# Two heads split at once, and doubled or laid over by transfers inside SBUF: the keys and queries of a two-layer decoder kernel

## The chip, the cores and the metric

The kernel runs on one core of one Trainium2 chip. The metric is the device time of one execution in microseconds, smaller is better; three executions are compared by their median. The chip is trn2 throughout. The engines are TensorE (PE in the rows; PEld is its weight load), VectorE (DVE), ScalarE (ACT), GpSimd (POOL) and SyncE (SP, which here issues the transfers).

## What is computed

Two layers of a hybrid decoder on one sequence of 512 tokens, 1024 wide, in fp32. Each layer projects the normalized input to three groups of heads of 64: 4 heads of forgetting attention, 8 query heads of native sparse attention (NSA, on 2 key groups, with compressed, selected and window branches) and 4 heads of dilated attention. Cut to what matters here:

```python
proj = h @ w_in
(fq, fk, fv, ff, nq, kc, vc, ks, vs, kw, vw, ng, dq, dk, dv) = jnp.split(proj, splits, axis=-1)
o_fox = fox_attention(heads(fq, 4), heads(fk, 4), heads(fv, 4), log_f)
o_nsa = nsa_attention(rope(nq, 8), rope(kc, 2), ..., rope(ks, 2), ..., rope(kw, 2), ...)
o_dil = dilated_attention(rope(dq, 4), rope(dk, 4), heads(dv, 4))
x = x + rms_norm(concat(o_fox, o_nsa, o_dil) @ w_out, attn_post_norm)
x = x + rms_norm(conv_ffn(rms_norm(x, ffn_pre_norm), ...), ffn_post_norm)
```

Scores are `q . k * 64**-0.5`, then masks, softmax and values.

## The kernel before

Tokens lie in four blocks of 128 (`NST`). Every factor of a matmul that must be exact is split into a high and a low part, each in the reduced fp32 form that TensorE takes at its full rate: `hi` is a rounding copy on ScalarE, `lo = x - hi` is a subtraction on VectorE (for some weights on GpSimd). A projection is hi·hi + hi·lo + lo·hi, in blocks of 12 matmuls (`s_mms`, through `mm` at line 115). Weights of a layer come in by loads of 512 KB that SyncE issues (`load`, line 134) into a pool of three raw tiles.

A score needs the product of a query head (64 channels) with a key head. The 128 rows of the array hold the query twice over, its high part in partitions 0 to 63 and its low part in 64 to 127; a key head is therefore needed **doubled**, the same 64 channels in both halves, and in two planes, high and low. A score is then two matmuls (`st_scores`): query tile by high plane, query tile by low plane.

How the tiles come about: a projection leaves tokens on partitions. `staged` (lines 718 to 743) copies each token block to a row buffer with the rotary turn (`rope`, lines 465 to 477); for keys it writes every head twice, side by side. `turn` (735 to 738) transposes 128 columns of the four token blocks into one PSUM tile, four transposes of 128x128 (tag `pt`, two buffers). For queries such a block holds two heads, for keys one head doubled. `keep` then calls `q_evac` (485 to 492: for each of the two heads one ScalarE copy of 64x512 with the scale into the upper half of the tile and one VectorE subtraction into the lower half) or `k_evac` (494 to 498: one ScalarE copy and one VectorE subtraction of 128x512 for the one doubled head). The forgetting heads' keys `fk` (525 to 543) are made in the same way, through `t_block` (479 to 483), and their queries `fq` straight from a projection that leaves channels on partitions, with `q_evac`.

Row buffers (`rt`) come from one pool of ten, which the attention rows of the units below use too.

The order around the change: the scores are cut into units (lines 1074 to 1079) of one head, branch and query block: units 0 to 15 forgetting, 16 to 79 NSA (head 0 branch `ks` is 16 to 19, head 0 branch `kw` 20 to 23), 80 to 95 dilated. The slot loop (1240 to 1251) runs one unit per slot through nine stages, each with its lag (`LAGS`), and between them takes `step`s of the projections still open, at the rate of a fixed table (`RATE`), on which pieces such as `evac`, `turn` and `keep` hang with delays (`EV`). `operands` (1081), called first in `st_scores`, takes steps until the query and key tiles of its unit are there (`until`, 1074). TensorE's order is this order of the program.

Of the kernel before, what the change touches and what calls it, by code (L numbers as in the profile page):

```python
# [10 lines left out]
F32R = mybir.dt.float32r  # L11
# [63 lines left out]
def tile_hybrid_block(  # L75
# [26 lines left out]
    def bt(shape, dt=F32, name="b"):  # L102
        return big.tile(shape, dt, tag="b", name=nm(name))
# [344 lines left out]
    for l in range(DEPTH):  # L448
# [43 lines left out]
            return q  # L492

        def k_evac(p):
            k = bt([128, 2, 512], F32R, "k")
            nc.scalar.activation(k[:, 0, :], p, AF.Copy)
            nc.vector.tensor_sub(k[:, 1, :], p, f(k[:, 0, :]))
            return k

        def new_v(nh=2):  # L500
            return bt([128, 8 // nh, nh, 2, 64], F32R, "v")
# [23 lines left out]
        for s in range(NST):  # L525
            if s % 2 == 0:
                for c in range(2):
                    for u in range(s, s + 2):
                        s_mms(sl256(pk_, u), u, range(4 * c, 4 * c + 4), wk[c], c == 0 and u % 2 == 0,
                              c == 1 and u % 2 == 1)  # L530
            p = ps("s")[:, 0:284]
            for c, (k0, k1) in enumerate(((0, 3), (3, 6), (6, 8))):
                s_mms(p, s, range(k0, k1), wv[c], c == 0, c == 2)
            if s == 1:
                turn_pair(1, 0, l, HT2)
            v_evac(fv[s // 2], s % 2, p[:, 0:256])
            nc.vector.tensor_add(zz[:, s, :], p[:, 256:284], bias)
            d = rt((128, 4, 2, 64))
            nc.scalar.activation(d, bc(hd(sl256(pk_, s)), 2, 2), AF.Copy)
            tl.append(d.rearrange("p h u d -> p (h u d)"))  # L540
        tmode.__exit__(None, None, None)
        store["fv"] = fv
        store["fk"] = [k_evac(t_block(tl, 128 * j)) for j in range(4)]
        cpar = small.tile([128, 2, 88], F32, tag="cpar", bufs=1, name=nm("cpar"))
        crow = rt((88, 2, 128))
        for j in range(3):
# [171 lines left out]
        def staged(key, turned, dup, nh, v=None, plain=0):  # L718

            tl = []  # L720

            def evac(s, p):
                w = nh * 64 * (2 if dup else 1)
                d = rt((128, w + plain))
                rope(d[:, 0:w].rearrange("p (h u d) -> p h u d", h=nh, d=64), hd(p[:, 0:64 * nh]), s, nh)
                if plain:
                    nc.scalar.activation(d[:, w:w + plain], p[:, 64 * nh:64 * nh + plain], AF.Copy)
                if v is not None:
                    if s == 0:
                        store[v] = new_v()  # L730
                    v_evac(store[v], s, p[:, 64 * nh:64 * nh + 128])
                tl.append(d)

            def turn(j):
                p = ps(TT)
                for s in range(NST):
                    nc.tensor.transpose(p[:, 128 * s:128 * s + 128], tl[s][:, 128 * j:128 * j + 128], ident)  # L737
                pieces.later(EV[3], keep, p)

            def keep(p):  # L740
                store.setdefault(key, []).append((k_evac if dup else q_evac)(p))

            return evac, [(turn, j) for j in range(nh * (2 if dup else 1) // 2)]

        def dv_evac(s, p):
            if s == 0:
# [353 lines left out]

        state, whole = {"o": None, "p": None}, []

        def st_scores(u):
            t = u["t"]
            n = u["n"] = 128 * (t + 1)
# [131 lines left out]
        with tc.manual_schedule(engines={mybir.EngineType.PE}):  # L1237
            for i in range(FIRST):
                step()
            for i in range(len(units) + LO):  # L1240
                slot[0] = i
                U = lambda lag: units[i - lag] if 0 <= i - lag < len(units) else None
                for lag, fn in stages:
                    if U(lag) is not None:
                        fn(U(lag))
# [177 lines left out]
```

## Time and profile before

| what | us |
|---|---|
| median of 3 runs (1368.1 to 1369.65) | 1369.39 |
| the profiled execution's own time | 1369.85 |
| its span | 1367.9 |
| mean granted TensorE clock | 0.998 of full |

The profile is of one execution. Its time stands 1.95 us above its span and 0.46 us above the median. The span has per layer one stage of projections and attention (about 40 to 310 us in layer 0, 710 to 985 us in layer 1) and one of output projection and feed-forward. The page gives engine totals, the chain that ended last and the costliest groups; the timelines, the waits and the transfers tell where in the program something happens.

### The profile page before, as it was taken

What the parts mean: (1) busy time and instruction counts of PE and PEld (TensorE: products, weight loads), DVE (VectorE), ACT (ScalarE), POOL (GpSimd) and SP (SyncE); (2) the same over time, 40 slices, a digit from 0 to 9 for tenths busy, and PEclk for the clock granted to TensorE, in tenths of its full rate; (3) what the DMA queues carried; (4) which work ended last, traced back from release to release, by engine and by line L of the source; (5) the groups of instructions that cost most, each with busy time, mean ns of one, the idle gap of its engine ahead of it and who ended that gap; (6) DMA issues with size and microseconds to landing.
All of it is one profiled execution on the core that took longest, in us unless ns stands there. A gap on an engine that the chain in (4) does not pass through costs nothing.

```text
span 1367.9 us, 21028 instructions
## 1 busy us (share of the span) xinstructions
PE 1338.0 (98%) x7855; PEld 1177.9 (86%) x7855; DVE 850.4 (62%) x1893; ACT 728.2 (53%) x1506; POOL 287.0 (21%) x343
## 2 busy tenths in 40 slices
PE   9999999999999999999999999999999999999997
PEld 8899998978888888888898999999798888888886
DVE  7677787677755555433464887777876555554334
ACT  6567767777533333333465677667774333333232
POOL 2364753341000000000004647634210000000000
PEclk9999999999999999999999999999999999999999
DMA  6323311131333333333333242111323333332231
GB/s 181 94 63 115 104 35 48 58 128 33 107 93 103 97 92 96 104 93 123 111 96 93 63 139 63 47 41 58 120 62 98 103 92 93 104 97 92 94 122 62
DMA packets 145517, 123.74 MB, mean 90 GB/s; under 512 B 8264, under 2 KB 135688, under 8 KB 145416
## 3 DMA queue, kind: packets, MB, share of 16 engines
q1 hardware_dynamic: 145416, 122.40, 29.5%
q8 instruction: 62, 1.02, 0.3%
q14 instruction: 39, 0.32, 0.1%
HBM read 118.19 MB, written 4.19 MB: 89 GB/s over the span
## 4 chain that ended last, share of the span: by engine, by line
PE 85%; DVE 7%; ACT 4%; POOL 2%; issue 2%; DMA 0%; SPq 0%; ACTq 0%; POOLq 0%; DVEq 0%
PE acc L115 39%; PE s L115 19%; PE pt L115 13%; PE o L115 10%; PE pt L1156 3%; POOL wt L795 1%; PE pt L737 1%; DVE hl L271 1%; DVE pl L1172 1%; DVE r L1126 1%; ACT r L1131 1%; DVE x L913 0%; ACT hh L270 0%; ACT h L310 0%; ACT ph L1167 0%
## 5 line engine op out<-in xcount | busy, mean ns | idle before, releaser
L154 DVE TENSOR_TENSOR wl_up<-raw_up,wh_up 128x1024 fp32r<-128x1024 f32 x78 | 95.6, 1225 | 170.8 <-ACT wh_up L146 170.8
L146 ACT ACTIVATE wh_up<-raw_up 128x1024 fp32r<-128x1024 f32 (+1 forms) x90 | 89.6, 1001 | 160.4 <-PE acc L115 68.1
L154 DVE TENSOR_TENSOR wl_wd<-raw_wd,wh_wd 128x1024 fp32r<-128x1024 f32 x42 | 51.5, 1225 | 133.7 <-ACT wh_wd L146 133.7
L146 ACT ACTIVATE wh_wd<-raw_wd 128x1024 fp32r<-128x1024 f32 x42 | 44.5, 1060 | 144.8 <-PE pt L115 135.5
L1143 POOL TENSOR_SCALAR r<-r,sm,gates 128x128 f32<-128x128 f32 (+3 forms) x128 | 86.4, 683 | 126.1 <-DVE sm L1139 82.3
L1131 ACT ACTIVATE r<-r,sm 128x128 f32<-128x128 f32 x192 | 106.7, 557 | 9.3 <-DVE sm L1126 8.4
L115 PE MATMUL acc<-hh,wl_up 128*128 128x512 f32 (+1 forms) x272 | 102.4, 376 | 0.0
L115 PE MATMUL acc<-hl,wh_up 128*128 128x512 f32 (+1 forms) x272 | 102.4, 376 | 0.0
L115 PE MATMUL acc<-hh,wh_up 128*128 128x512 f32 (+1 forms) x272 | 102.4, 376 | 0.0
L150 POOL TENSOR_TENSOR wl_kc<-raw_kc,wh_kc 128x512 fp32r<-128x512 f32 x8 | 11.8, 1490 | 417.6 <-ACT wh_kc L146 416.8
L115 PE MATMUL s<-k,q 128*128 128x512 f32 (+3 forms) x384 | 96.2, 337 | 0.6 <-DVE sm L1126 0.6
L1172 DVE TENSOR_TENSOR pl<-pt,ph 128x384 fp32r<-128x384 f32 x144 | 85.6, 596 | 17.3 <-ACT ph L1167 15.9
L1167 ACT ACTIVATE ph<-pt 128x384 fp32r<-128x384 f32 x144 | 75.4, 523 | 29.1 <-PE pt L1156 27.9
L1126 DVE CUSTOM_DVE_ANT_0 r<-s,cmask 128x128 f32<-128x128 f32 (+3 forms) x160 | 76.0, 482 | 20.6 <-PE s L115 16.2
L1156 PE MATMUL pt<-ident,r 128*128 128x128 f32 x480 | 77.5, 276 | 7.0 <-DVE pl L1172 5.5
L115 PE MATMUL acc<-wh_wd,gh 128*128 128x512 f32 x252 | 83.7, 389 | 0.0
L115 PE MATMUL s<-hh,wh_up 128*128 128x512 f32 (+1 forms) x224 | 80.4, 359 | 0.0
L115 PE MATMUL s<-hl,wh_up 128*128 128x512 f32 (+1 forms) x224 | 80.4, 359 | 0.0
L115 PE MATMUL s<-hh,wl_up 128*128 128x512 f32 (+1 forms) x224 | 80.4, 359 | 0.0
L1347 ACT ACTIVATE r<-r 128x512 f32<-128x512 f32 x44 | 27.8, 632 | 85.7 <-DVE r L1328 85.5
L1156 PEld LDWEIGHTS pt<-ident,r 128*128 128x128 f32 x480 | 55.4, 141 | 15.9 <-POOL r L1143 6.8
L115 PE MATMUL acc<-wh_wo,mix 128*128 128x256 f32 (+1 forms) x296 | 67.6, 305 | 0.0
(439 smaller groups left out, 4121.2 us busy)
## 6 DMA issues: line engine op xcount, KB each, us to landing
raw_up<-in_w_up_dram SPq DMA_DIRECT2D x88, 512.0 KB, 3.8
raw_wd<-in_w_down_dram SPq DMA_DIRECT2D x44, 512.0 KB, 3.4
raw_wo<-in_w_out_dram SPq DMA_DIRECT2D x16, 512.0 KB, 3.5
x<-in_x_dram SPq DMA_DIRECT2D x8, 512.0 KB, 5.9
raw_nq<-in_w_in_dram SPq DMA_DIRECT2D x8, 512.0 KB, 3.7
raw_w<-in_cmp_w_k_dram SPq DMA_DIRECT2D x8, 512.0 KB, 4.0
raw_w<-in_cmp_w_v_dram SPq DMA_DIRECT2D x8, 512.0 KB, 4.2
raw_fk<-in_w_in_dram SPq DMA_DIRECT2D x4, 512.0 KB, 5.9
```

What stands on the lines that cost most here:

```text
L115: nc.tensor.matmul(o, lhsT=lhsT, rhs=rhs, start=start, stop=stop, skip_group_check=True)
L146: nc.scalar.activation(hi[:, ks], raw[:, ks], AF.Copy)
L154: nc.vector.tensor_sub(lo[:, ks], raw[:, ks], f(hi)[:, ks])
L271: nc.vector.scalar_tensor_tensor(lo, src, gain[:, k:k + 1], f(hi), op0=ALU.mult, op1=ALU.subtract)
L737: nc.tensor.transpose(p[:, 128 * s:128 * s + 128], tl[s][:, 128 * j:128 * j + 128], ident)
L1126: nc.vector.tensor_tensor_reduce(row[:, 0:n], u["S"][:, 0:n], u["mask"][:, 512 - n:512], op0=ALU.add, op1=ALU.min, scale=1.0, scalar=3.0e3 ...
L1131: nc.scalar.activation(row[:, 0:n], row[:, 0:n], AF.Exp, scale=-1.0, bias=sm_[0], accum_out=sm_[1])
L1143: nc.gpsimd.tensor_scalar(row[:, 0:n], row[:, 0:n], z["sm"][2], g_, op0=ALU.mult, op1=ALU.mult)
L1156: nc.tensor.transpose(p[:, 128 * c:128 * c + 128], blocks[z], ident)
L1167: nc.scalar.activation(hi, src, AF.Copy)
L1172: nc.vector.tensor_sub(*u["lo"])
L1347: nc.scalar.activation(cd[0], cd[0], AF.Silu)
```

## The change

Keys are no longer written twice side by side: the row buffers of `fk` and of `staged` hold each head once, a turned block holds two key heads, and half as many key blocks are turned. `k_evac` makes two key tiles from one block: one ScalarE copy and one VectorE subtraction of 128x512 into the second tile, then three transfers of 64x1024 (256 KB each) on SyncE's queue: the first head from the upper half of the second tile to both halves of the first, and then the second head from its lower half to its upper half. `q_move` replaces `q_evac` for the NSA and dilated queries: one ScalarE copy and one VectorE subtraction of 128x512 into two row buffers, then four transfers of 64x512 (128 KB each) that lay high and low parts of the two heads over each other in the query tile; `fq` keeps `q_evac`. `ask` takes the steps for the operands of a unit with the first query block one slot earlier, for NSA and dilated units.

```diff
--- before.py
+++ after.py
@@ -492,10 +492,26 @@
             return q
 
         def k_evac(p):
-            k = bt([128, 2, 512], F32R, "k")
-            nc.scalar.activation(k[:, 0, :], p, AF.Copy)
-            nc.vector.tensor_sub(k[:, 1, :], p, f(k[:, 0, :]))
+
+            k = [bt([128, 2, 512], F32R, "k") for _ in range(2)]
+            own, other = slice(64, 128), slice(0, 64)
+            nc.scalar.activation(k[1][:, 0, :], p, AF.Copy)
+            nc.vector.tensor_sub(k[1][:, 1, :], p, f(k[1][:, 0, :]))
+            for h in (other, own):
+                nc.sync.dma_start(f(k[0])[h], f(k[1])[other])
+            nc.sync.dma_start(f(k[1])[other], f(k[1])[own])
             return k
+
+        def q_move(p):
+
+            hi, lo = rt(dt=F32R), rt(dt=F32R)
+            nc.scalar.activation(hi, p, AF.Copy, scale=-0.125)
+            nc.vector.scalar_tensor_tensor(lo, p, -0.125, f(hi), op0=ALU.mult, op1=ALU.subtract)
+            q = bt([128, 2, 512], F32R, "q")
+            for j in range(2):
+                for i, part in enumerate((hi, lo)):
+                    nc.sync.dma_start(f(q)[64 * i:64 * i + 64, j, :], f(part)[64 * j:64 * j + 64, :])
+            return [q]
 
         def new_v(nh=2):
             return bt([128, 8 // nh, nh, 2, 64], F32R, "v")
@@ -535,12 +551,12 @@
                 turn_pair(1, 0, l, HT2)
             v_evac(fv[s // 2], s % 2, p[:, 0:256])
             nc.vector.tensor_add(zz[:, s, :], p[:, 256:284], bias)
-            d = rt((128, 4, 2, 64))
-            nc.scalar.activation(d, bc(hd(sl256(pk_, s)), 2, 2), AF.Copy)
-            tl.append(d.rearrange("p h u d -> p (h u d)"))
+            d = rt((128, 256))
+            nc.scalar.activation(d, sl256(pk_, s), AF.Copy)
+            tl.append(d)
         tmode.__exit__(None, None, None)
         store["fv"] = fv
-        store["fk"] = [k_evac(t_block(tl, 128 * j)) for j in range(4)]
+        store["fk"] = [k for j in range(2) for k in k_evac(t_block(tl, 128 * j))]
         cpar = small.tile([128, 2, 88], F32, tag="cpar", bufs=1, name=nm("cpar"))
         crow = rt((88, 2, 128))
         for j in range(3):
@@ -720,7 +736,7 @@
             tl = []
 
             def evac(s, p):
-                w = nh * 64 * (2 if dup else 1)
+                w = nh * 64
                 d = rt((128, w + plain))
                 rope(d[:, 0:w].rearrange("p (h u d) -> p h u d", h=nh, d=64), hd(p[:, 0:64 * nh]), s, nh)
                 if plain:
@@ -738,9 +754,9 @@
                 pieces.later(EV[3], keep, p)
 
             def keep(p):
-                store.setdefault(key, []).append((k_evac if dup else q_evac)(p))
-
-            return evac, [(turn, j) for j in range(nh * (2 if dup else 1) // 2)]
+                store.setdefault(key, []).extend((k_evac if dup else q_move)(p))
+
+            return evac, [(turn, j) for j in range(nh // 2)]
 
         def dv_evac(s, p):
             if s == 0:
@@ -1100,6 +1116,11 @@
 
         state, whole = {"o": None, "p": None}, []
 
+        def ask(u):
+            if u["t"] == 0 and u["grp"] != "f":
+                operands(u)
+
+
         def st_scores(u):
             t = u["t"]
             n = u["n"] = 128 * (t + 1)
@@ -1240,6 +1261,8 @@
             for i in range(len(units) + LO):
                 slot[0] = i
                 U = lambda lag: units[i - lag] if 0 <= i - lag < len(units) else None
+                if i + 1 < len(units):
+                    ask(units[i + 1])
                 for lag, fn in stages:
                     if U(lag) is not None:
                         fn(U(lag))
```

How the change moves instructions, at three places of layer 0. The first is TensorE around the first score of unit 16 (`s<-k,q` with the query tile of the first two NSA heads; `kw` is the projection of the window keys, L737 in the program before and L753 in the changed one are the transposes of `turn`). Before:

```order
L115 MATMUL acc_1525<-wh_kw_229_1365,hl_94 128x256
L737 MATMUL pt_1598<-ident,r_1417 128x128
L737 MATMUL pt_1598<-ident,r_1449 128x128
L737 MATMUL pt_1598<-ident,r_1498 128x128
L737 MATMUL pt_1598<-ident,r_1546 128x128
L115 MATMUL s_1608<-k_1341,q_1603 128x128 x2
L115 MATMUL acc_1525<-wh_kw_229_1365,hh_89 128x256
L115 MATMUL acc_1525<-wl_kw_230_1366,hh_89 128x256
```

And now:

```order
L115 MATMUL acc_1494<-wh_kw_227_1356,hl_94 128x256
L753 MATMUL pt_1567<-ident,r_1405 128x128
L753 MATMUL pt_1567<-ident,r_1437 128x128
L753 MATMUL pt_1567<-ident,r_1486 128x128
L753 MATMUL pt_1567<-ident,r_1515 128x128
L115 MATMUL s_1581<-k_590,q_720 128x512 x2
L115 MATMUL s_1581<-cst,esel 128x512
L1177 MATMUL pt_1595<-ident,r_1382 128x128 x4
L115 MATMUL s_1600<-k_1328,q_1576 128x128 x2
L115 MATMUL acc_1494<-wh_kw_227_1356,hh_89 128x256
```

The second turn of the NSA queries now comes ahead of the scores of unit 15 (three matmuls into `s_1581`) and of the transposes of four rows (L1177), and unit 16's score, which read its query straight behind the turn, now comes behind these. Between the first turn and the second stand 12 matmuls of `kw` in both.

The second place is SyncE's queue in the same part of the program, with the loads of weights (`raw_w` of the compression, `raw_nq` of the second half of the NSA queries). Before:

```order
L134 DMA raw_w_0_2_286_1650<-in_cmp_w_k_dram 128x4x256
L134 DMA raw_w_0_3_298_1694<-in_cmp_w_k_dram 128x4x256
L134 DMA raw_nq_0_309_1753<-in_w_in_dram 128x4x256
L134 DMA raw_w_1_0_316_1809<-in_cmp_w_v_dram 128x4x256
L134 DMA raw_w_1_1_324_1838<-in_cmp_w_v_dram 128x4x256
L134 DMA raw_nq_1_329_1876<-in_w_in_dram 128x4x256
L134 DMA raw_w_1_2_357_2000<-in_cmp_w_v_dram 128x4x256
L134 DMA raw_w_1_3_364_2028<-in_cmp_w_v_dram 128x4x256
```

And now:

```order
L134 DMA raw_w_0_3_299_1690<-in_cmp_w_k_dram 128x4x256
L513 DMA q_1576<-r_1572 64x512
L513 DMA q_1576<-r_1573 64x512
L513 DMA q_1576<-r_1572 64x512
L513 DMA q_1576<-r_1573 64x512
L513 DMA q_1628<-r_1624 64x512
L513 DMA q_1628<-r_1625 64x512
L513 DMA q_1628<-r_1624 64x512
L513 DMA q_1628<-r_1625 64x512
L134 DMA raw_nq_0_305_1731<-in_w_in_dram 128x4x256
L134 DMA raw_w_1_0_312_1787<-in_cmp_w_v_dram 128x4x256
L134 DMA raw_w_1_1_320_1816<-in_cmp_w_v_dram 128x4x256
```

The transfers of keys (L501, L502) and queries (L513) stand between the loads: the load of `raw_nq` now comes behind eight of them, which wait for ScalarE's and VectorE's halves of two query pairs.

The third place is TensorE around unit 20, the first with window keys (`w_1_0` is a weight of the compression, `nq` the second half of the NSA query projection). Before:

```order
L115 MATMUL acc_1875<-wl_w_1_0_326_1841,wth_1383 128x256
L737 MATMUL pt_1892<-ident,r_1744 128x128
L737 MATMUL pt_1892<-ident,r_1769 128x128
L737 MATMUL pt_1892<-ident,r_1801 128x128
L737 MATMUL pt_1892<-ident,r_1825 128x128
L115 MATMUL s_1900<-k_1897,q_1603 128x128 x2
L115 MATMUL s_1900<-k_1897,q_1603 128x256 x2
L1156 MATMUL pt_1921<-ident,r_1639 128x128
L1156 MATMUL pt_1921<-ident,r_1672 128x128 x2
```

And now (L1177 is the transposes of the rows; between the two pieces stand eleven more matmuls of `nq`):

```order
L115 MATMUL acc_1853<-wl_w_1_0_322_1819,wth_1374 128x256
L115 MATMUL acc_1853<-wh_w_1_0_321_1818,wth_1374 128x256
L115 MATMUL acc_1853<-wl_w_1_0_322_1819,wth_1374 128x256
L115 MATMUL s_1877<-k_1328,q_1576 128x512 x2
L1177 MATMUL pt_1890<-ident,r_1604 128x128 x4
L115 MATMUL acc_1815<-wh_nq_0_313_1789,hh_89 128x256
L115 MATMUL acc_1815<-wl_nq_0_314_1790,hh_89 128x256
L115 MATMUL acc_1815<-wh_nq_0_313_1789,hl_93 128x256
...
L115 MATMUL acc_1815<-wl_nq_0_314_1790,hh_90 128x256
L115 MATMUL acc_1815<-wh_nq_0_313_1789,hl_94 128x256
L115 MATMUL s_1907<-k_1870,q_1576 128x128 x2
```

The first score of unit 20 stood right behind the second turn of the window keys. There is one turn now, further ahead, and between it and that score stand the matmuls with `w_1_0`, the scores of unit 19, four transposes and twelve matmuls of `nq`.

## Rows read from the trace of the kernel before

**Rows 1.** The page, part 1: busy time, its share of the span and the number of instructions of each engine.

```profile
PE 1338.0 (98%) x7855; PEld 1177.9 (86%) x7855; DVE 850.4 (62%) x1893; ACT 728.2 (53%) x1506; POOL 287.0 (21%) x343
```

**Rows 2.** The page, part 4: the chain of work that ended last, shares of the span by engine.

```profile
PE 85%; DVE 7%; ACT 4%; POOL 2%; issue 2%; DMA 0%; SPq 0%; ACTq 0%; POOLq 0%; DVEq 0%
```

**Rows 3.** The waits of TensorE over the whole span: who waited, for whom, microseconds in total, how many times, the longest.

```profile
PE pt L1156 <- DVE pl L1172: 5.5, 6, 1.5
PE pt L1156 <- DVE mx L1221: 1.0, 2, 0.5
PE pt L552 <- DVE k L497: 0.9, 1, 0.9
PE acc L115 <- DVE q L490: 0.6, 1, 0.6
PE pt L1156 <- DVE k L497: 0.4, 2, 0.2
PE pt L115 <- DVE q L490: 0.3, 2, 0.2
```

**Rows 4.** The instructions of the lines 482 and 737 (the transposes), 490 (subtraction of a query half) and 497 (subtraction of a key): how many, their shortest, median and longest duration in ns, first and last start, shape.

```profile
L482 PE MATMUL pt<-ident,r x32: 270/272/318, 39.9 to 718.4; 128*128 128x128 f32 x32
...
L737 PE MATMUL pt<-ident,r x112: 270/273/328, 92.4 to 922.7; 128*128 128x128 f32 x112
...
L490 DVE SCALAR_TENSOR_TENSOR q<-pt,q x24: 683/690/695, 111.3 to 897.2; 64x512 fp32r<-64x512 f32 x24
...
L497 DVE TENSOR_TENSOR k<-pt,k x24: 619/685/692, 42.3 to 923.9; 128x512 fp32r<-128x512 f32 x24
```

**Rows 5.** The timeline of TensorE around the first score of the first NSA unit, layer 0: start, duration, what. A start is the beginning of the group, the duration ends with its last result, so groups overlap.

```profile
109.91 0.60 PE L737 MATMUL pt<-ident,r 128*128 128x128 f32 x4
110.27 0.36 PE L115 MATMUL acc<-wh_kw,hh 128*128 128x256 f32 x1
110.47 0.28 PE L115 MATMUL acc<-wl_kw,hh 128*128 128x256 f32 x1
...
111.78 0.60 PE L737 MATMUL pt<-ident,r 128*128 128x128 f32 x4
112.14 0.42 PE L115 MATMUL s<-k,q 128*128 128x128 f32 x2
```

**Rows 6.** The same timeline a little earlier: scores and transposes of the last forgetting unit and its neighbours.

```profile
104.93 0.63 PE L115 MATMUL s<-k,q 128*128 128x512 f32 x2
105.40 0.40 PE L115 MATMUL s<-cst,esel 128*128 128x512 f32 x1
105.64 0.60 PE L1156 MATMUL pt<-ident,r 128*128 128x128 f32 x4
105.99 0.37 PE L115 MATMUL acc<-wh_kw,hh 128*128 128x256 f32 x1
```

**Rows 7.** The timeline of ScalarE in the stretch of rows 5; the number in brackets is idle time before, with what ended it.

```profile
111.22 0.62 ACT L146 ACTIVATE wh_kw<-raw_kw 128x512 fp32r<-128x512 f32 x1
```

**Rows 8.** The timeline of TensorE around the first score of unit 20 (the first with window keys), layer 0.

```profile
128.77 0.84 PE L737 MATMUL pt<-ident,r 128*128 128x128 f32 x4
...
130.42 0.60 PE L737 MATMUL pt<-ident,r 128*128 128x128 f32 x4
130.78 0.87 PE L115 MATMUL s<-k,q 128*128 128x128 f32 x4
```

**Rows 9.** The timelines of ScalarE and VectorE in the same stretch: the split of the first window key block.

```profile
129.66 0.60 ACT L496 ACTIVATE k<-pt 128x512 fp32r<-128x512 f32 x1 [0.25 <-PE pt L737]
...
130.29 0.69 DVE L497 TENSOR_TENSOR k<-pt,k 128x512 fp32r<-128x512 f32 x1 [0.28 <-ACT k L496]
```

**Rows 10.** The timeline of SyncE's queue, layer 0: loads as they are issued (start, time from the first issue to the end of the last, what).

```profile
127.17 1.97 SPq L134 DMA_DIRECT2D raw_w<-in_cmp_w_v_dram  x2
...
162.17 0.46 SPq L765 DMA_DIRECT2D w2r<-in_cmp_w_v_dram  x1
```

**Rows 11.** Transfers: what, queue, how many, KB of one, and median microseconds from issue to landing; the first row is of the stretch from 105 to 135 us alone, the others of the whole span (xsv and out are written from SBUF, the others read into it).

```profile
raw_w<-in_cmp_w_v_dram SPq DMA_DIRECT2D x4, 512.0 KB, 3.8
...
raw_fk<-in_w_in_dram SPq DMA_DIRECT2D x4, 512.0 KB, 5.9
...
xsv<-x SPq DMA_DIRECT2D x4, 512.0 KB, 4.4
...
out_dram<-x SPq DMA_DIRECT2D x4, 512.0 KB, 2.6
...
posr<-in_cmp_pos_v_dram SPq DMA_DIRECT2D x2, 8.0 KB, 2.2
```

**Rows 12.** Busy time of each engine in one stretch of 2 us of layer 1 (with the number of instructions in brackets; PEclk is the granted clock of TensorE, 1.00 is its upper level), and two rows of the chain that ended last: the same 12 projection matmuls in layer 0 and in layer 1.

```profile
894.00:896.00 2.00, 1.80 (x9) 1.83 (x10) 0.86 (x6) 1.89 (x6) 1.20 (x1) 0.50 0.65 233
...
220.13 1.44 PE acc L115 x12
...
895.07 2.53 PE acc L115 x12
```

**Rows 13.** The longest wait of TensorE behind VectorE in layer 0, and VectorE in the microseconds before it.

```profile
166.27 0.52 PE L1156 MATMUL pt<-ident,r 128*128 128x128 f32 x3 [1.52 <-DVE pl L1172]
...
164.11 0.69 DVE L490 SCALAR_TENSOR_TENSOR q<-pt,q 64x512 fp32r<-64x512 f32 x1
...
165.44 0.69 DVE L1172 TENSOR_TENSOR pl<-pt,ph 128x512 fp32r<-128x512 f32 x1
```

## The prediction

> **What bounds the kernel now.** I read the page's totals first: TensorE is busy for 1338.0 of 1367.9 us, VectorE for 850.4, ScalarE for 728.2 [rows 1]. The chain that ended last says the same: 85% of the span is TensorE, 0% a transfer [rows 2]. So only two things count: what TensorE no longer has to issue, and the short waits in which it stands. Work taken from VectorE and ScalarE counts where one of these waits ends on it. The waits [rows 3] name VectorE's query and key subtractions at a few places; the timelines show what TensorE does around the scores whose operands will come by transfer [rows 5, 6, 8].
>
> **a. Transposes removed: −5.3 us.** Half the key blocks go: per layer 2 of `fk`, one of `ks`, one of `kw`, 2 of `dk`, 12 blocks of 4 transposes in all; line 482 falls from 32 to 16, line 737 from 112 to 80 [rows 4]. Their median of 0.27 us each would make 13 us, but a duration contains the pipeline: four start at 109.91, the next matmul at 110.27, and that one takes 0.20 to its successor [rows 5] where 12 of its kind take 1.44, or 0.12 each [rows 12]. A block costs 0.36 + 0.08 = 0.44 us, 12 of them 5.3.
>
> **b. Waits behind VectorE: −4.3 us.** Twelve key and twelve query subtractions of 0.685 and 0.690 go [rows 4], 16.5 us of VectorE, and as many copies of about 0.6 [rows 9], some 14 us, of ScalarE. The waits that name them are 0.9 (L552 behind the fourth `fk` block), 0.4 and 0.3 [rows 3]; I take them as gone, 1.6. The 0.6 (`acc` behind a query) belongs to `fq`, which keeps its code; the shorter VectorE queue ahead of it should give half, 0.3. The 1.0 behind `mx` stands right behind a query subtraction and weight work: gone. Of the 5.5 behind `pl`, the two longest, one per layer, stand behind a queue in which another query's subtraction, 0.69 at 164.11, is one of three pieces before `pl` at 165.44 [rows 13]: half of 1.52 twice, less a little, 1.4. Sum 4.3, between 1.5 (only the named ones) and 6.
>
> **Clock: −1.1 us.** In layer 1 alone the granted clock shows 0.50 from 894 to 896, its lower level (1.2 of 2.4 GHz), after TensorE had waited at 891, 892 and 894 in turn, and 12 matmuls take 2.53 where the same dozen in layer 0 takes 1.44 [rows 12]. These waits are those of b behind `dq`; if they go, so does the 1.1.
>
> **c. New waits, +8.6 us.** A key or query head now reaches its score through a transfer, and every transfer is hidden where TensorE has other work until then. At two places per layer it has not.
>
> *Place A, the first NSA score.* From the start T of the first query turn (109.91 before), TensorE now issues the turn 0.36, 12 `kw` matmuls 1.51 [rows 5], the second turn 0.36 and 0.08, unit 15's three scores 0.71 and its transposes 0.35 [rows 6]: it wants the query at T+3.4. ScalarE first finishes the second `kw` weight half; the one whole copy takes the place of 111.22, T+1.3 [rows 7], and ends at T+1.95, the subtraction 0.69 later at T+2.65. Then the transfer. No row shows one inside SBUF. From the issue to the landing the nearest take 2.6 (512 KB out of SBUF with nothing else running), at least 2.2 (8 KB) and 4.4 (512 KB out of SBUF among other loads) [rows 11]. Only 128 KB move and no load is ahead that has not landed: I take 2.6. It lands at T+5.25, a wait of 1.9 (1.5 to 3.7).
>
> *Place B, unit 20.* From the start T' of the one turn left (128.77), the path is the turn 0.62 and 8 matmuls 1.03, that is 1.65 to the start of what was the second turn [rows 8], unit 19's scores 0.47 and transposes 0.35 [rows 6], 12 `nq` matmuls 1.51: it wants the keys at T'+4.0. The split ends at 130.98, T'+2.2 [rows 9]; two transfers of 256 KB fill the first key tile, the second issued about 0.4 later. Two loads of 512 KB were issued at 127.17 and by 129.14, just ahead of them [rows 10], and loads of this stretch land after 3.8 [rows 11]; I take 3.8: T'+6.4, a wait of 2.4 (1.2 with 2.6; 4.5 with the 5.9 of `raw_fk` [rows 11]).
>
> Both in both layers: 2 × (1.9 + 2.4) = 8.6, between 5.4 and 16.4. The Trainium skill, "DMA: Bandwidth & Descriptors", section "Anatomy of one DMA — SWDGE (gpsimd) path", fits a fixed 2.0 us plus bytes by 436 GB/s; an estimate by it is 2.3 us for 128 KB and 2.6 for 256 KB, and the four waits would come to 5.5. Its fit is for another issuing path than SyncE's, and the loads here land later than it says (it gives 3.2 for 512 KB; the stretch shows 3.8), so the row decides.
>
> **Costed at nothing.** The 84 transfers, 42 a layer, each some 0.46 us of SyncE's queue like the load at 162.17 [rows 10], move loads back: `raw_nq` by under 2 us, before ScalarE wants it. Keys and queries of `fk`, `dq`, `dk` are split many microseconds ahead of their first score, with one or two dozen matmuls per slot between. The second pair of NSA queries of `nq1` stands behind loads that end with 162.17 [rows 10]; its two row buffers come free only when the transfers land, and VectorE's row maximum takes them next. The reciprocals around 163 keep VectorE busy until about then; without that cover it is 2 us a layer. Taking operands a slot early moves blocks of 12, adding none.
>
> **The sum.** −5.3 − 4.3 − 1.1 + 8.6 = −2.1 on the profiled execution's 1369.85 (span and what lies around it): 1367.75. That execution stands 0.46 above the median of the runs, so 1367.3 against 1369.39. About 0.2%, 2.7 us, is what a measurement of this kernel can tell from no change.
>
> **Rivals.**
> 1. *The transfers are quick and the relief whole.* Landing at the lower bounds, waits 5.4, and all 6 of b: −5.3 − 6.0 − 1.1 + 5.4 = −7.0, 1362.4. For it: 512 KB from SBUF land in 2.6 when alone. Against it: loads run beside them.
> 2. *Each new wait drops the clock.* The dip of layer 1 came behind pauses shorter than these [rows 12]. If each of the four new waits costs a dozen matmuls at the lower level, 4 × 1.1 comes back: +2.3, 1371.7. Against it: the 1.52 at 166.27 [rows 13] was followed by matmuls at 0.12.
> 3. *Slower: the moves between halves run at half rate.* Each transfer starts and ends in 64 partitions. From 8 KB at 2.2 to 512 KB at 4.4 [rows 11] is 0.55 us per 128 KB; at half the rate 1.1. At A two parts go (+2.2): landing after 4.4, a wait of 3.65; at B two moves (+4.4): 6.6, a wait of 4.8. Together 2 × 8.45 = 16.9, the sum +6.2: 1375.6. It decides from waits of 13.4 in sum, 3.35 each, where the sum passes +2.7. Against it: `out` at 2.6. For it, by itself: the Trainium skill, "SBUF — State Buffer", section "Door 1: The DMA port swizzle (why [64,N] ≈ [32,N])", says that 64 adjacent partitions reach only 8 of 16 ports. No run here shows that yet.
> That the change doesn't do what it says is excluded: the transposes counted in a are gone from TensorE's order.
>
> **Chances.** Forecast 0.47, its own range 1364.5 to 1370 from the bounds 1.5 to 6 of b and 7 to 10 of c: its middle lies above the faster bound of 1366.7, 0.22 of it is faster and 0.25 the same. Rival 1: 0.15, faster. Rival 2: 0.16, the same (1372.1 is the bound). Rival 3: 0.22, slower. Faster 0.37, same 0.41, slower 0.22. The range 1362.0 to 1374.0 holds the forecast, rival 2, rival 1 but for its quicker half and of rival 3 the part with waits up to 15.3; about 0.2 lie outside.
>
> **What would show it.** TensorE: 16 and 80 transposes; the gaps of L552 and behind `q` gone from its waits; instead four waits of about 2 us at `s<-k,q`, put down to a transfer, 3.4 behind the first turn and 4.0 behind the window keys' turn in each layer. VectorE down by some 16 us and ScalarE by some 14, with nothing gained from it beyond b. Layer 1 at 894: clock 1.00. Transfers: `q<-r` 2.6, `k<-k` 3.8 from issue to landing. I am wrong on c if these waits are below 1 us or above 3.4; on a if twelve blocks save less than 4 us between the same marks; on b if the waits behind `pl` stay at 5.5; on the cover if TensorE waits where `nq1` or the dilated heads begin.

## The result: 1385.65 us, slower by 1.2%

The changed kernel takes 1385.65 us (median of four runs, 1382.77 to 1389.28) against 1368.82 before on the same chip: 1.0124 times as long, 95% interval 1.0098 to 1.0150. The forecast was 1367.3, in a range of 1362.0 to 1374.0. The profiled execution took 1389.28, the slowest of the four; its span is 1387.5. The runs now lie 6.5 us apart where those before lay 1.6 apart.

The totals and the chain of the changed kernel; they answer to [rows 1] and [rows 2].

```profile
PE 1339.4 (97%) x7807; PEld 1179.5 (85%) x7807; DVE 839.7 (61%) x1869; ACT 711.8 (51%) x1482; POOL 284.9 (21%) x343
...
PE 80%; DVE 8%; ACT 6%; POOL 2%; issue 2%; DMA 1%; SPq 0%; ACTq 0%; POOLq 0%; DVEq 0%
```

VectorE lost 10.7 us of work where I had counted 16.5 and ScalarE 16.4 where I had counted 14; the kernel is slower all the same. TensorE issues 48 instructions less, but its share of the chain fell from 85 to 80%. What it waits for (in total, times, longest), to be held against [rows 3]:

```profile
PE s L115 <- DMA k<-k: 8.8, 2, 4.7
PE acc L1055 <- DVE sm L1046: 5.5, 2, 2.9
PE pt L1177 <- DVE pl L1193: 3.1, 4, 0.9
...
PE pt L1177 <- DVE k L499: 2.2, 2, 1.1
PE s L115 <- DVE sm L1160: 2.2, 1, 2.2
...
PE s L115 <- DVE r L509: 1.6, 1, 1.6
```

The wait for `k<-k` is unit 20's, in both layers. The first NSA query's wait shows under VectorE's names (`DVE r L509` in layer 0, `DVE sm L1160` in layer 1): VectorE's part had ended by then and the transfer was what came last, as the timelines show below (in the fourth and sixth run, further down, such a wait has the name `DMA q<-r`). The two at L1055 (transposes of the compressed branch) and L1177 behind `k L499` (0.4 before) were not in my sum. The transposes of the compressed branch waited before, too, but for less:

```profile
PE acc L1039 <- DVE pcl L1047: 1.3, 2, 0.7
```

Line by line, the transposes that answer to [rows 4] are as counted:

```profile
L482 PE MATMUL pt<-ident,r x16: 270/272/273, 39.8 to 723.3; 128*128 128x128 f32 x16
...
L753 PE MATMUL pt<-ident,r x80: 272/273/330, 90.1 to 933.4; 128*128 128x128 f32 x80
```

**Place A**, the first NSA score of layer 0: TensorE's timeline, then VectorE's subtraction of the first query pair, then SyncE's queue. It answers to [rows 5 to 7].

```profile
105.88 0.60 PE L753 MATMUL pt<-ident,r 128*128 128x128 f32 x4
...
108.88 0.60 PE L1177 MATMUL pt<-ident,r 128*128 128x128 f32 x4
111.09 0.41 PE L115 MATMUL s<-k,q 128*128 128x128 f32 x2 [1.61 <-DVE r L509]
...
107.75 0.69 DVE L509 SCALAR_TENSOR_TENSOR r<-pt,r 128x512 fp32r<-128x512 f32 x1 [2.05 <-ACT r L508]
...
107.67 5.37 SPq L513 DMA_DIRECT2D q<-r  x8
```

From the turn at 105.88 the rest went as forecast: TensorE came for the query at T+3.35, the subtraction ended at T+2.56, the eight issues began at 107.67, and the score started at T+5.2, 1.6 us late by the row (1.9 forecast). In layer 1 it was 2.2.

**Place B**, unit 20 of layer 0, in the same way (turn, last matmul of `nq` and score; VectorE's subtraction; SyncE's queue with the two loads ahead and the two key moves). It answers to [rows 8 to 10].

```profile
126.82 0.73 PE L753 MATMUL pt<-ident,r 128*128 128x128 f32 x4
...
130.58 0.28 PE L115 MATMUL acc<-wh_nq,hl 128*128 128x256 f32 x1
135.60 0.66 PE L115 MATMUL s<-k,q 128*128 128x128 f32 x2 [4.74 <-DMA k<-k]
...
128.22 0.69 DVE L499 TENSOR_TENSOR k<-pt,k 128x512 fp32r<-128x512 f32 x1
...
125.21 1.96 SPq L134 DMA_DIRECT2D raw_w<-in_cmp_w_v_dram  x2
128.93 1.11 SPq L501 DMA_DIRECT2D k<-k  x2
```

The split ended at 128.9, T'+2.1, and TensorE had no more work at T'+3.9, both as forecast. But the second move, issued at about 129.5, landed only when the score started at 135.60, after some 6.1 us instead of 3.8: 4.74 us of waiting in layer 0 and 4.05 in layer 1, where I had 2.4.

**The clock** fell behind most of these waits. Granted clock (the column after the five engines) in two stretches of 2 us, and three dozens of projection matmuls on the chain; they answer to [rows 12].

```profile
136.00:138.00 2.00, 2.00 (x11) 2.00 (x11) 0.65 (x5) 0.53 (x2) 0.00 (x0) 0.50 0.61 133
822.00:824.00 2.00, 2.00 (x12) 2.00 (x11) 0.73 (x2) 0.99 (x5) 0.71 (x2) 0.50 0.00 0
...
137.44 2.13 PE acc L115 x12
...
821.60 2.56 PE acc L115 x12
...
891.63 2.67 PE acc L115 x12
```

0.50 is the lower level, 1.2 GHz. A dozen takes 2.13, 2.56 and 2.67 us there instead of 1.44: after unit 20 in both layers and, in layer 1, behind the 2.88 us of waiting at the compressed branch (890.65), a few microseconds ahead of where the old dip stood. Behind place A of layer 1 the clock is 0.50 from 795 to 797; behind place A of layer 0, and behind the 2.58 us at the compressed branch of layer 0, it stayed at 1.00.

### The profile page after: what moved, and what is told of

Its sections match the earlier page's. It is cut to its first block, busy times and chain, and to the rows that moved or that the text cites. A ratio compares the mean times of both kernels' runs of the same rounds, so it can differ in the third digit from the quotient of the medians.

```text
span 1387.5 us, 21128 instructions
## 1 busy us (share of the span) xinstructions
PE 1339.4 (97%) x7807; PEld 1179.5 (85%) x7807; DVE 839.7 (61%) x1869; ACT 711.8 (51%) x1482; POOL 284.9 (21%) x343
## 4 chain that ended last, share of the span: by engine, by line
PE 80%; DVE 8%; ACT 6%; POOL 2%; issue 2%; DMA 1%; SPq 0%; ACTq 0%; POOLq 0%; DVEq 0%
PE acc L115 37%; PE s L115 18%; PE pt L115 12%; PE o L115 9%; PE pt L1177 3%; ACT r L1152 1%; DVE hl L271 1%; DVE pl L1193 1%; DMA k<-k 1%; ACT ph L1188 1%; POOL wt L811 1%; DVE wt L811 1%; ACT hh L270 1%; PE pt L753 1%; ACT r L1226 0%
## 5 line engine op out<-in xcount | busy, mean ns | idle before, releaser
L1152 ACT ACTIVATE r<-r,sm 128x128 f32<-128x128 f32 x192 | 106.9, 558 | 20.3 <-DVE sm L1147 19.3
L115 PE MATMUL s<-k,q 128*128 128x512 f32 (+3 forms) x384 | 97.6, 342 | 12.6 <-DMA k<-k 8.8
L1177 PE MATMUL pt<-ident,r 128*128 128x128 f32 x480 | 78.8, 278 | 8.5 <-DVE pl L1193 3.1
L115 PEld LDWEIGHTS s<-k,q 128*128 128x128 f32 x384 | 59.7, 197 | 16.8 <-issue 12.1
L1177 PEld LDWEIGHTS pt<-ident,r 128*128 128x128 f32 x480 | 56.0, 142 | 17.9 <-POOL r L1164 6.9
```

What stands on the lines that cost most here:

```text
L115: nc.tensor.matmul(o, lhsT=lhsT, rhs=rhs, start=start, stop=stop, skip_group_check=True)
L1152: nc.scalar.activation(row[:, 0:n], row[:, 0:n], AF.Exp, scale=-1.0, bias=sm_[0], accum_out=sm_[1])
L1177: nc.tensor.transpose(p[:, 128 * c:128 * c + 128], blocks[z], ident)
```

## The experiments

Every kernel was compared with the kernel before on the same chip; the times are medians.

**1. Transfers alone.** No edit of the kernel, but a program of its own.

> This kernel computes nothing of the layers; it makes transfers one kind at a time, six times each, with the engines idle: 64x1024 (256 KB, 64 partitions to the other 64) alone; 128x1024 (512 KB) and 128x512 (256 KB) over all partitions; two of 64x1024 from one half, as a key tile is filled; 64x512 (128 KB); a load of 512 KB alone; and two loads of 512 KB with two of 64x1024 right behind. Theory 1 (the key moves landed 6 us after their issue because loads stand ahead of them in the same queues): alone 64x1024 takes 2.6 to 3.0, two take 3.3 to 3.8, and behind two loads about 6. Theory 2 (moves between the halves run at half rate): 64x1024 alone takes clearly longer than 128x512 of the same size, 3.2 against 2.6 or more, and the two alone already 4.5 or more.

Its transfers: kind, queue, how many, KB of one, median microseconds from issue to landing (`one`: 64x1024 from one half to the other; `two`: two from one half, one to each half, as a key tile is filled; `behind`: two such right behind two loads; `half`: 128x512; `full`: 128x1024; `low`: 64x512; `ld`: the loads, 6 alone and 12 in pairs). It was run once, with six rounds.

```profile
ld<-in_w_in_dram SPq DMA_DIRECT2D x18, 512.0 KB, 3.7
full<-src SPq DMA_DIRECT2D x6, 512.0 KB, 2.9
two<-src SPq DMA_DIRECT2D x12, 256.0 KB, 3.2
behind<-src SPq DMA_DIRECT2D x12, 256.0 KB, 6.5
...
one<-src SPq DMA_DIRECT2D x6, 256.0 KB, 2.8
half<-src SPq DMA_DIRECT2D x6, 256.0 KB, 2.3
low<-src SPq DMA_DIRECT2D x6, 128.0 KB, 2.2
```

Theory 1 is borne out: two key moves land after 3.2 us with nothing else running (it gave 3.3 to 3.8) and after 6.5 behind two loads. A cost of the 64 partitions is seen too, but is small: 2.8 against 2.3 for the same 256 KB, and 2.9 for twice the bytes over all partitions. That agrees in kind with the Trainium skill, "SBUF — State Buffer", section "Door 1: The DMA port swizzle (why [64,N] ≈ [32,N])", by which a half of the partitions reaches only 8 of the 16 ports; here it is worth 0.5 us. It is too little for unit 20's delay. The other page weighed in the prediction, "DMA: Bandwidth & Descriptors" of the Trainium skill, section "Anatomy of one DMA — SWDGE (gpsimd) path", has a fit for another issuing path; an estimate by it is 2.3 us for 128 KB and 2.6 for 256 KB: the quiet 2.2 and 2.8 are near it, the 6.5 is not in it. In this program the moves are issued right behind the loads, in the kernel some 2 to 4 us behind them, so the 6.5 is a neighbour of the kernel's case and not the case itself. In the changed kernel itself the same rows read:

```profile
k<-k SPq DMA_DIRECT2D x36, 256.0 KB, 4.4
...
q<-r SPq DMA_DIRECT2D x48, 128.0 KB, 2.3
```

**2 and 3. Keys alone, queries alone.** The edit of the second was

```diff
-                store.setdefault(key, []).extend((k_evac if dup else q_move)(p))
+                store.setdefault(key, []).extend((k_evac if dup else (lambda p: [q_evac(p)]) if qk in ('nq0', 'nq1', 'dq') else q_move)(p))
```

(`qk` names the projection; the three names are all that `staged` makes queries for), and the third took back everything on keys (doubled rows, one head per block, no key moves).

> Queries are split by the engines as in the kernel before; keys and the earlier request for operands stay as changed. Theory 1 (the loss is two places per layer, the first NSA query and the window keys, and a later wait of the compressed branch that comes from the queries' transfers): the first place is gone, unit 20 still waits 4 to 5 us per layer and the clock falls behind it, the compressed branch does not wait 2.7 at its transposes: 1373 to 1376. Rival (the compressed branch's wait and the clock come from the changed order and not from the queries): 1381 to 1385.

> Keys are doubled by the engines as in the kernel before; queries and the earlier request for operands stay as changed. Theory 1: the wait of about 2 us at the first NSA score stays in both layers, unit 20 does not wait, the compressed branch waits 2.7 per layer: 1377 to 1381. Rival (compressed branch not from the queries): 1372 to 1375.

Measured: 1382.26 (ratio 1.0100, 1.0083 to 1.0117) and 1381.24 (1.0095, 1.0080 to 1.0110). The second came out where its rival stood, the third just over theory 1's range; together they cannot add: 14 and 13 us over the kernel before, where both in one kernel cost 17. The places were as expected, the sizes not quite: unit 20 waited 3.5 and 3.7 us in the second, the first NSA query 1.3 and 1.2 in the third. Both traces had the 2.6 us at the compressed branch's transposes and the 1.1 behind the dilated keys, in each layer. What they share is the early request.

**4. Window keys by the engines**, all else as changed: `staged` writes doubled rows for `nkw` and `keep` takes the old `k_evac` for it.

> Only the window keys are doubled by the engines again; all else as changed. Theory 1: the time falls by the two waits of 4.9 and 4.2 us at unit 20 and the lowered clock behind them, some 12 us in all: 1372 to 1375. Rival (the wait moves on to the next transfer that is short of cover, so that little comes back): 1380 or more.

1375.09 (1.0049, 1.0034 to 1.0064), 10.6 us less than the changed kernel, at the upper edge of what theory 1 gave for this place.

**5 and 6. The early request alone, and everything but it.** The fifth is the kernel before with `ask` and its call; the sixth the changed kernel without the call:

```diff
-                if i + 1 < len(units):
-                    ask(units[i + 1])
```

> The kernel before, with the earlier request for operands alone; keys and queries are made by the engines as before, and no transfer is added. The two runs with keys or queries alone both waited 2.7 us per layer at the compressed branch's transposes and 1.1 behind the dilated keys, which neither theory of the transfers gave to both. New theory (the earlier request shifts the whole order of projections and units, and costs 4 to 6 us per layer by itself): 1376 to 1382, with both of these waits and a lowered clock in layer 1. Rival (these waits come from what queries and keys share, the row buffers, the queue of transfers and VectorE's order): 1367 to 1371.

> The changed kernel without the earlier request. New theory: the compressed branch's wait and that behind the dilated keys go (some 10 us), while the first NSA query has 1.1 us and the window keys 2.3 us less cover per layer, with more lowered clock: 1379 to 1385, with waits near 3 and 7 us at the two places. Rival (the request costs nothing of itself): 1390 to 1396.

1378.05 (1.0067, 1.0052 to 1.0082) and 1385.95 (1.0134, 1.0117 to 1.0151). Without a single transfer added, the request alone costs 9.6 us. Its waits (TensorE, total, times, longest):

```profile
PE acc L1062 <- DVE sm L1053: 5.2, 2, 2.6
...
PE pt L1184 <- DVE k L508: 2.2, 2, 1.1
PE pt L1184 <- DVE q L490: 2.2, 2, 1.1
```

The first two are the waits that the second and third run share; the third arises in the request's own slot. The lowered clock in layer 1, which I had expected with them, is not there: it is 1.00 through both attention stages. And taking the request out of the changed kernel gives nothing in the median: the window keys then wait 5.7 and 4.7 and the first query 2.8 and 2.4. It bought about as much cover as it cost; that is no more than a rough balance, as the sixth's runs reach from 1382.04, the profiled one, to 1389.96.

**7 and 8. Keys with a long lead.** Early request and query moves out; new keys for `fk` alone, and for `fk`, `ks` and `dk`.

> The kernel before with the forgetting heads' keys alone made two heads at once and doubled by transfers. In the changed kernel layer 0 reached the first matmul of kc 2.1 us early and layer 1 gained 2.4 by the same point. New theory (keys with a long lead keep that gain to the end): 1363 to 1365. Rival (the gain is given back at the next wait on another engine): 1366 to 1368.

> The kernel before with the forgetting, the selected and the dilated keys made in the new way, window keys and all queries as before, no earlier request. New theory: four waits of transfers are not there, 10 blocks of transposes go (4.4 us) and the waits behind VectorE's key subtractions (2 to 3 us): 1361 to 1363.5. Rival (a transfer is late at the dilated heads or at the first selected unit, or the moves delay the loads behind them): 1366 or more.

1364.85 (0.9972, 0.9962 to 0.9983) and 1363.00 (0.9957, 0.9942 to 0.9971): both as the new theory said, 3.6 and 5.5 us faster than before. The fifth, too, lay in its range; the sixth stands 1 us above it.

**9. One step paid back ahead of unit 20.** Counted in TensorE's order, the projection matmuls ahead of a unit's first score are these:

```
unit          15    16    19    20    40    79    80    81
before       384   428   460   544   724  1096  1108  1120
changed      428   428   544   556   736  1108  1120  1120
```

At unit 20 the request takes the missing steps one slot early, the loop's budget hands out its own step as before, and from there to unit 80 every unit has 12 matmuls more ahead of it: projections and units stand one step apart from where they did. The edit:

```diff
                     ask(units[i + 1])
+                    if i + 1 == 20:
+                        budget -= 1.0
```

> The changed kernel, with one step of projection taken out of the slot loop's budget right after the early request for unit 20. From unit 20 on, each unit then has as many projection matmuls ahead of it as in the kernel before; in the changed kernel it has 12 more, to the end of the layer. Theory 3 (the early request costs by this shift of 12 matmuls alone: units and projections meet GpSimd and VectorE in another order, and 1.4 us less are left to fill the end): the waits at the compressed branch's transposes and behind the dilated keys fall back to below 1 us and the end of the stage gains 2 us per layer: 1375 to 1379, with the waits at the first NSA query and unit 20 unchanged. Rival (the request costs where it is made): 1383 or more.

1382.02 (1.0104, 1.0087 to 1.0121), between the two. The wait at the compressed branch fell back to the old 1.3 as theory 3 said. Behind the dilated keys the 1.1 is gone, but four shorter waits make 2.3 in sum, no less than in the changed kernel. And this edit takes the 12 matmuls from just ahead of unit 20, whose wait rose to 4.9 and 4.8 us though its keys landed sooner in this run. So I did it again behind that score (13 to 15).

**10 to 12. What may be moved.** Early request out; window keys and first NSA query half by the engines; 10: keys of 8 with queries of `nq1` and `dq` by transfer; 11: keys of 8 with `dq`; 12: `fk` and `ks` alone.

> Keys of the forgetting, selected and dilated heads and the queries of the second NSA half and the dilated heads in the new way; window keys and the first NSA half by the engines, no early request. Theory 1: only tiles with long cover are moved, and VectorE's and ScalarE's relief shortens the waits around 166 and 219: 1360.5 to 1363. Rival (the queries' row buffers are held until the transfers land, and VectorE's row maximum waits for them): 1365 or more, with waits behind `r` of the queries in layer 0 and 1.

> As the run with long-lead keys, with the dilated queries by transfer in addition. Theory 1: the 0.7 behind `mx` per layer goes and the rest stays: 1361 to 1363. Rival (row buffers): 1364 or more.

> As the run with long-lead keys, but the dilated keys by the engines as before. In that run the first matmul of wo stood 3.05 and the last 2.55 us ahead in layer 0, so the dilated keys gave nothing there beside a new wait of 1.1; in layer 1 the lowered clock at 894 was absent. Theory 1 (dilated keys gain only by that clock): 1363 to 1364.5. Rival (two blocks of transposes and VectorE's relief count): 1365 or more.

1362.46 (0.9959, 0.9944 to 0.9974), 1362.36 (0.9957, 0.9942 to 0.9972) and 1364.05 (0.9968, 0.9957 to 0.9979). All three lie where theory 1 put them. For 11 that is partly luck, since the wait behind `mx` that was to go grew (see below). The cover of `nq1` holds: no wait in 10 is put down to a transfer. Numbers 8, 10 and 11 lie too close for their intervals to order them. They are the fastest versions, 5.5 to 5.7 us ahead of the kernel before.

**13 to 15. The step paid back behind unit 20's score.** To the early request alone, to 4, and to the changed kernel:

```diff
-                budget += RATE[i]
+                budget += RATE[i] - (1.0 if i == 20 else 0.0)
```

> The kernel before with the early request alone, as in the run that took 1378.05, but one step of projection is taken out of the budget in the slot of unit 20, behind its score; from unit 22 on, the projections stand against the units as in the kernel before. Theory 3 (the request costs by the shift of 12 matmuls that it leaves to the end of the layer): the waits of 2.7 and 1.1 us go, only the 1.25 at the last forgetting unit's transposes stays per layer: 1369.5 to 1372. Rival (the request costs where it is made, in slots 15 and 19): 1375 or more.

> As the run with window keys by the engines (1375.09), with that step taken out. If the shift and the window keys' wait are separate and add: 1366.5 to 1370. If what the shift costs is hidden under the transfers' waits: 1372 or more.

> The changed kernel with the step taken out behind unit 20's score instead of ahead of it, so that its window keys keep their 12 matmuls of cover (the run with the step taken out ahead took 1382.02). Theory: 1.5 us less wait per layer, 1377 to 1380.5. Rival (the landing of the window keys moves with what the loads do, and the cover does not decide): 1381 to 1384.

1370.25 (1.0015, 1.0005 to 1.0024), 1366.75 (0.9984, 0.9975 to 0.9994) and 1377.48 (1.0062, 1.0047 to 1.0077). In the thirteenth the wait at the transposes of the compressed branch is the old one behind `pcl`, and only what the request does in its own slot stays:

```profile
PE pt L1184 <- DVE q L490: 2.2, 2, 1.1
...
PE acc L1062 <- DVE pcl L1070: 1.3, 2, 0.6
```

The shift of one step thus costs 7.8 us alone (1378.05 to 1370.25), 8.3 without the window keys' moves (1375.09 to 1366.75) and 8.2 in the changed kernel (1385.65 to 1377.48): it is separate and it adds. Each taken over the kernel before on its own chip, the three are 7.8, 8.7 and 7.8; the first is the firmest, as the runs of 5 and 13 lie within 1 and 2 us and those of the changed kernel within 6.5. In the fifteenth the waits for transfers are left (place A of layer 0 waits 1.5):

```profile
PE s L115 <- DMA k<-k: 7.5, 2, 3.9
...
PE s L115 <- DVE sm L1160: 2.1, 1, 2.1
```

Of the 7.8 between 5 and 13, the waits at the compressed branch make 3.9 (5.2 against 1.3), those behind the dilated keys 1.8, and those behind `pl` at the transposes 2.7 (11.7 against 9.0), less some small ones that go the other way. How the shift costs at the compressed branch is read from the changed kernel's timelines, one engine after another, as a chain in time (POOL, DVE, ACT, DVE, PE); it was not tried by itself.

```profile
198.00 2.53 POOL L150 TENSOR_TENSOR wl_dk<-raw_dk,wh_dk 128x512 fp32r<-128x512 f32 x2
...
202.03 0.73 POOL L1044 TENSOR_TENSOR r<-r,cvalid 128x256 f32<-128x256 f32 x1
...
202.80 0.42 DVE L1045 TENSOR_REDUCE sm<-r 128x8 f32<-128x256 f32 x1 [1.68 <-POOL r L1044]
203.14 0.55 DVE L1147 CUSTOM_DVE_ANT_0 r<-s,cmask 128x384 f32<-128x384 f32 x1
...
203.73 0.61 ACT L1152 ACTIVATE r<-r,sm 128x384 f32<-128x384 f32 x1 [1.04 <-DVE sm L1147]
...
204.74 0.42 DVE L1063 TENSOR_TENSOR pcl<-acc,pch 128x256 fp32r<-128x256 f32 x1
...
205.31 0.41 PE L1055 MATMUL acc<-ident,r 128*128 128x128 f32 x2 [2.58 <-DVE sm L1046]
```

GpSimd now does both halves of a `dk` weight one behind the other (2.53 us) ahead of the row of the compressed branch; before, they stood apart:

```profile
191.20 1.29 POOL L150 TENSOR_TENSOR wl_dk<-raw_dk,wh_dk 128x512 fp32r<-128x512 f32 x1
...
194.71 1.29 POOL L150 TENSOR_TENSOR wl_dk<-raw_dk,wh_dk 128x512 fp32r<-128x512 f32 x1
```

VectorE sits idle 1.68 us for that row, and the unit's row maximum, its exponential and the evacuation of `pch` and `pcl` stand behind it in the order of their queues; TensorE's transposes come 2.6 us late. The order comes and goes with the shift: in 5 the two halves stand together as well (2.54 us from 193.26), and in 13, with the step paid back, they are apart again (1.29 at 191.91 and 1.28 at 195.41).

## Why the prediction was wrong

**The step that failed first** is the sentence "Taking operands a slot early moves blocks of 12, adding none". It adds none, but the blocks stay a step ahead of the units to unit 80, and GpSimd's and VectorE's pieces then come in another order. Costed at nothing, measured some 8 us (8.2 from the changed kernel to 15, 7.8 from 5 to 13), nearly half of the miss of 18. I had looked at the order around places A and B and not behind them. The rest of what I costed at nothing held: no other wait of TensorE in the changed kernel is put down to a transfer, at `nq1` or the dilated heads either.

**c, the new waits.** The places, the path and the split times were right at both, and A's wait too (1.6 and 2.2, forecast 1.9). B's term was mis-sized: 4.7 and 4.05 us instead of 2.4, since the moves landed 5.4 to 6.1 after their issue and not 3.8; I took the landing of a load for that of two moves behind two loads (1 shows 6.5 right behind them). The four waits make 12.6 us where I had 8.6. And three of them came with the lower clock (not A of layer 0), which I had put into a rival by itself: window keys by the engines give 10.7 us back (15 to 14), of which the waits are 7.5.

**The clock's −1.1** did not come in the changed kernel, whose shift put a wait of 2.88 us near the same place. Its ground was wrong, too. In 7, where dilated keys and queries are made as before, the same three waits of 0.47, 0.17 and 0.53 us stand in layer 1, the last of them at 889.47, and the clock stays at its upper level; from the first to the last matmul of `dk`, layer 1 gains 1.5 us on the kernel before and layer 0 nothing. The last of the three waits, and a stretch of 2 us behind it with the granted clock after the five engines (it is 1.00 from 886 to 890, too):

```profile
889.47 0.52 PE L1184 MATMUL pt<-ident,r 128*128 128x128 f32 x3 [0.53 <-DVE mx L1249]
...
890.00:892.00 2.00, 2.00 (x16) 1.96 (x16) 0.94 (x2) 1.95 (x7) 1.29 (x1) 1.00 0.55 219
```

So these waits do not decide it, and I had taken one execution's dip for every execution's: of the ten runs of the kernel before that stand beside 5 to 8, seven show a mean granted clock of 0.999 and take 1367.95 to 1368.76, three 0.997 or 0.998 and 1369.44 to 1369.73. The profiled one shows 0.998 and takes 1369.85. In most runs there was then little or nothing of the 1.1 to win.

**a, the transposes**, held: counts as said. In 8 and 11, ten of the 12 blocks are gone and TensorE's waits are in sum what they were (21.7 and 21.9 us against 21.4 before); they gain 5.5 and 5.7 us, where ten blocks at 0.44 make 4.4.

**b, VectorE's relief**, was too large. The 0.9 and the 0.6 before `kc` went (with them 7 gains 3.6 where four blocks make 1.8). The rest is read from 11, which moves the dilated queries but leaves `nq1`'s to the engines, and from 10, which moves both; nothing is shifted in either (total, times, longest; 11 first):

```profile
PE pt L1184 <- DVE pl L1200: 5.6, 6, 1.5
PE pt L1184 <- DVE k L499: 2.3, 4, 0.9
...
PE pt L1184 <- DVE mx L1249: 1.9, 2, 0.9
```

```profile
PE pt L1184 <- DVE pl L1200: 3.0, 4, 1.1
PE pt L1184 <- DVE r L515: 2.3, 2, 1.1
```

The two long waits of 1.52 behind `pl` stay where `nq1`'s queries are not moved; where they are, two waits of 1.15 behind the moved queries' own subtraction (`r L515`) stand in their place: 0.7 us won where I had 1.4. The 1.0 behind `mx` grew to 1.9 in both runs, and the dilated keys' subtraction, now one for two heads, gave 2.3 in place of 0.4. What came of the 4.3 is eaten up by these two: TensorE's waits are 21.9 us in sum in 11 and 20.3 in 10. So even a change without A, B and the request ends near −6 and not at the −10.7 that a, b and the clock made. VectorE's busy time fell by less than counted because the shift itself lengthens it: 5, with as many instructions as before, shows 856.8 us against 850.4.

**The forecast's own range**, 1364.5 to 1370, is not what its bounds give: with 6 of b and 7 of c it is 1364.0, with 1.5 and 10 it is 1371.5. The measured time lies far above either.

**The rivals.** "Slower" came true, at 0.22, but not by its mechanism: the 64 partitions cost 0.5 us a move (1). That its price at B (4.8) was met is luck: the moves were late by something else, most likely the loads ahead. The clock's rival was true in kind. That two causes add, each on the slower side, stood in no case of mine.

The parts in order of the medians: the changed kernel 1385.65; without the shift 1377.48 (−8.2); window keys by the engines too 1366.75 (−10.7); first NSA query half by the engines and no request at all 1362.46 (−4.3); and what is left is 5.6 us faster than the kernel before beside it.

**What stays open:** why the second move took 6.1 us in the changed kernel's profile and 3.8 to 5.3 in those of 6, 9 and 15, with the same loads ahead. It fits the wider spread of the runs, but no run tells what sets it. Nor does one tell when a wait lowers the clock: 2.2 us at place A of layer 1 did in the changed kernel and did not in 9.

## What to carry to other kernels

Where an order written by hand lets two streams of work run past each other, a step taken early must be taken out of the budget again, or the distance stays changed to the end; count the work ahead of each unit over the whole stage, not around the edit. A transfer in place of engine work pays where its tile has more work ahead of it than the landing behind the loads of that stretch (here some 4 to 6 us, not the 2 to 3 of a quiet queue), and costs the wait and the clock behind it where it has not.

## What the chip showed beyond that

Two moves inside SBUF that take 3.2 us alone take 6.5 behind two loads of 512 KB (run 1); such a load takes 3.5 to 3.8 alone and 4.7 to 5.1 in a pair. A move of 256 KB between the halves takes 2.8 us, over all partitions 2.3. The granted clock fell to its lower level behind waits of 4.7, 4.1, 2.9 and 2.2 us in the changed kernel's profile, but not behind the 1.6 us at place A and the 2.6 at the compressed branch of layer 0, nor behind either of the 2.6 in 5: the length of a single wait does not tell.
